# Room for four transpose tiles, another place for the first bias tiles, and an earlier fetch of the raw value weights at the end of a prologue

## The chip, the cores and the metric

The kernel runs on one core of one Trainium2 chip. The metric is the time of one execution in microseconds, as the device measures it; the median of several executions counts, and lower is better. Engines are called by name: TensorE (PE) multiplies matrices and transposes, VectorE (DVE), ScalarE (ACT) and GpSimd (POOL) do elementwise work, and SyncE (SP) issues most of the DMAs. All five run their own queue of instructions in order and meet through semaphores.

## The reference

One layer of a hybrid encoder, in float32, for a sequence of 2048 tokens of width 1024. The first norm feeds one projection; its first 512 columns go to a state-space layer, the rest are queries, keys and values of a chunked attention with a bias by relative distance.

```python
h = rmsnorm(x, norm_mix_g[l])
proj = h @ w_in[l]                      # 1024 -> u (512), q, k, v (512 each)
y_ssm = s5_mixer(u_ssm, lam, log_dt, b, c, d, w_glu, b_glu)
y_att = chunked_attention(q, k, v, rel_bias)     # 64-frame chunks, 8 chunks to the left
mixed = concat(rmsnorm(y_ssm, ...), rmsnorm(y_att, ...))
x = x + mixed @ w_out[l]
h2 = rmsnorm(x, norm_ffn_g[l])
x = x + (silu(h2 @ w_gate[l]) * (h2 @ w_up[l])) @ w_down[l]
return rmsnorm(x, norm_final_g)
```

## The kernel before

Everything is held feature by token: 128 features on the partitions, tokens along the row. Each float32 operand of a large product is split in two parts, `hi` (rounded) and `lo` (the rest), and a product is three matmuls (`mm3`): hi by hi, hi by lo, lo by hi. `split` makes the two parts of a weight: ScalarE casts `hi` out of a raw tile, VectorE or GpSimd subtracts it to get `lo`.

The stages follow one another: `u_phase` (the projection to u, in four pieces of 512 tokens, with the state-space constants of `ssm_prologue` computed between its steps), the attention with the state-space scan beside it (`att_phase`, four blocks of 512 tokens), the mixing, the gated FFN. Only the seam of the first two matters here, about 95 to 160 us into the run.

At that seam the following runs.

- `hT_unit(0)` loads the first block's input (`xt`, eight tiles of 128 by 512), scales it on VectorE and splits it into `hi` and `lo`. This happens in a callback `operands()` while TensorE still computes the last piece of u.
- VectorE then empties the last four accumulators of u (`us`), and GpSimd's queue writes them to memory (`u<-us`).
- `qk_unit(0, 0)` multiplies queries and keys of the first two heads (accumulators `pf`); its weights are tiles `w` split from `raw`.
- The rest of `ssm_prologue` follows: `bbg` and four `vg` are gathered from memory by SP, TensorE multiplies them (`pp<-vg,bbg`) into `kt`; then `transposes` turns the products `vw` in 16 pairs, ScalarE copies each pair to a tile `bst`, and GpSimd's queue writes each full `bst` (four pairs) to memory.
- `v_unit(0, 0)` multiplies values with weights n = 8 and n = 10; `scores` multiplies queries by keys into `sc`, adds the bias tile `nb` on VectorE and takes the minimum; `transp` turns the exponentials and stores them in `pth` and `ptl`.

The bias table `nbms` is written by `table()` from the small vector `nbs` and patched with `corner`; `nb` is one head's 128 by 640 piece of it.

What sets the order: TensorE's instructions, and those given through `k.V`, `k.A` and `k.Q` (VectorE, ScalarE, SyncE), keep their program order; the others are placed by a list scheduler. Tiles come from pools with a fixed count of buffers per tag (`bufs`). Two stacks of pools grow from both ends of the on-chip memory. A pool that is opened after another was closed lies over its room, and a write to a tile waits for every earlier reader and writer of the bytes below it. So the place of a tile decides what it waits for: `pk` (with `bst`, `vg`, `bbg`, `dm`, `kt`) lies over the tiles of `u_phase` on the right, and `aa` (with `nb`, `s`, `pth`, `ptl`) over those of the prologue (`vw` among them) on the left. Within `aa` the tiles lie in the order of their first use. All DMAs that SP issues go through one queue; each carries one of eight semaphores in turn and waits for the one eight before it.

Of the kernel before, what the change touches and what calls it, by code (L numbers as in the profile page):

```python
# [10 lines left out]
F32R = mybir.dt.float32r  # L11
# [5 lines left out]
P = 128  # L17
# [3 lines left out]
NG, CH, NS = 32, 16, 64  # L21
# [85 lines left out]
def f32(ap):  # L107
    return ap.bitcast(F32)
# [54 lines left out]
def split(k, hi, lo, raw, lo_eng=None, hi_eng=None):  # L163
    nc = k.nc
    (hi_eng or nc.scalar).copy(hi, raw)  # L165
    (lo_eng or nc.gpsimd).tensor_tensor(lo, raw, f32(hi), op=ALU.subtract)  # L166


def ssm_prologue(k, ident, S):

    tc, nc, io = k.tc, k.nc, k.io
    V = nc.vector
    with tc.tile_pool(name="pro", bufs=1) as p:
# [122 lines left out]
                eng.tensor_tensor(out, t1, t2, op=op)  # L296

        def transposes(pk, b_, wt):
            bst = k.t(pk, "bst", [P, 8, 2, NS], bufs=2)
            for q in range(4):  # L300
                ps = k.t(k.pro_psum, "pp", [P, 512])[:].rearrange("p (a b) -> p a b", a=4)
                for c in range(2):
                    k.te.transpose(ps[:, c, :], wt[c][:, q].rearrange("p j c -> p (j c)"), ident[:])
                nc.scalar.copy(bst[:, 2 * q : 2 * q + 2].rearrange("p g c n -> p c g n"), ps[:, :2].rearrange("p c (g n) -> p c g n", g=2))
                if q % 2:
                    yield
            nc.gpsimd.dma_start(S["bst"][b_], bst[:].rearrange("p g c n -> p (g c n)"))
# [8 lines left out]
        pr, pi = k.t(p, "pr", [P, NPR, 9]), k.t(p, "pi", [P, NPR, 9])  # L316
# [73 lines left out]
        pk = k.pk()  # L390
# [290 lines left out]
def att_phase(k, ident, S):  # L681
    tc, nc, io = k.tc, k.nc, k.io
    with ExitStack() as cx:
        aw = tc.alloc_tile_pool(name="aw", reuse_waits="tile", bufs=1, side="right")
        hT, vts, qk, keep = {}, {}, {}, {}

        def load_w(sb, n):

            w = k.t(aw, "w", [P, 2, 1024], F32R, bufs=WB)
            if sb == 0:  # L690
                raw = k.t(aw, "raw", [P, 1024], bufs=2)
                pin = n in (0, 4)
                (k.Q if pin else nc.sync).dma_start(raw[:], io["w_qk"][n] if n < 8 else io["w_v"][n - 8])
                split(k, w[:, 0], w[:, 1], raw[:], k.V if pin else k.wlo_eng, k.A if pin else None)
                keep[n] = w
            else:
                nc.sync.dma_start(f32(w[:]), S["ws"][n])
            return w[:, 0], w[:, 1]
# [5 lines left out]
        def hT_unit(sb, q0=0, q1=KT):  # L704
            hi, lo = hT.setdefault(sb, ([], []))
            ts = slice(sb * SB, (sb + 1) * SB)
            xts = {}
            V, A, Q = (k.V, k.A, k.Q) if sb == 0 else (nc.vector, nc.scalar, nc.sync)

            def load(q):  # L710
                if q < q1:
                    x = RING[q] if sb == 0 and q < 2 * DB else None
                    xts[q] = k.t(aw, x, [P, SB]) if x else k.t(aw, "xt", [P, SB], bufs=XB)
                    Q.dma_start(xts[q][:], io["xt"][q * P : (q + 1) * P, ts])

            ahead = 2 if sb else KT
            for q in range(q0, q0 + ahead):
                load(q)
            def low(q):
                V.tensor_tensor(lo[q][:], xts[q][:], f32(hi[q][:]), op=ALU.subtract)  # L720

            for q in range(q0, q1):
                yield
                load(q + ahead)
                xt = xts[q]
                for v, n in zip(hT[sb], ("hi", "lo")):
                    v.append(k.t(aw, f"{n}{q}x" if q < DB and sb % 2 else f"{n}{q}", [P, SB], F32R))
                V.scalar_tensor_tensor(xt[:], xt[:], k.gm[:, q : q + 1], S["rsn"][:, ts], op0=ALU.mult, op1=ALU.mult)
                A.copy(hi[q][:], xt[:])
                if sb == 0 and q:  # L730
                    low(q - 1)
                if sb or q == KT - 1:
                    low(q)
            yield

        def qk_unit(sb, pr):
            ws = [load_w(sb, n) for n in (pr, 4 + pr)]
            yield
            hi, lo = hT[sb]
# [42 lines left out]
        def v_unit(sb, fh):  # L782
            ws = [load_w(sb, 8 + 2 * r + fh) for r in range(2)]
            yield
            for i in range(4):
                vts[4 * sb + i, fh] = k.t(pv, f"v{fh}", [P, H // 2, 2 * HD], F32R)
            hi, lo = hT[sb]
            for i in range(4):
                ps = k.t(pfs, "pf", [P, 256])
                ic = slice(i * P, (i + 1) * P)  # L790
                for q in range(KT):
                    cs = slice((q % 4) * 256, (q % 4 + 1) * 256)
                    wh, wl = (w[:, cs] for w in ws[q // 4])
                    k.ta.matmul(ps[:], hi[q][:, ic], wh, start=q == 0, stop=False)
                    k.ta.matmul(ps[:], hi[q][:, ic], wl, start=False, stop=False)
                    k.ta.matmul(ps[:], lo[q][:, ic], wh, start=False, stop=q == KT - 1)
                    if q % 2 and q < KT - 1:
                        yield
                if i == 0:
                    for r in range(2):  # L800
                        keep_w(8 + 2 * r + fh)
                vt = vts[4 * sb + i, fh]
                pv3 = ps[:].rearrange("p (h d) -> p h d", h=4)
                nc.scalar.copy(vt[:, :, :HD], pv3)
                nc.vector.tensor_tensor(vt[:, :, HD:], pv3, f32(vt[:, :, :HD]), op=ALU.subtract)
                yield
# [45 lines left out]
        def transp(st):  # L852
            sb, pr, hh, qp = st
            hd = st_head[sb, 2 * pr + hh]
            if qp == 0:
                hd.p = k.t(aa, "pth", [P, 5, 4, P], F32R), k.t(aa, "ptl", [P, 5, 4, P], F32R)
            pth, ptl = hd.p
            s, k0 = hd.s.pop(qp)
            pt = k.t(psum, "pt", [P, 5, P], bufs=1)
            for kb in range(k0, qp + 5):  # L860
                k.ta.transpose(pt[:, kb % 5, :], s[:, (kb - k0) * P : (kb - k0 + 1) * P], ident[:])
            runs = [(0, 5)] if sb else ([(4, 5)] if qp == 0 else [(4, 5), (0, qp)])
            for a, b in runs:
                nc.scalar.copy(pth[:, a:b, qp, :], pt[:, a:b, :])
                nc.vector.tensor_tensor(ptl[:, a:b, qp, :], pt[:, a:b, :], f32(pth[:, a:b, qp, :]), op=ALU.subtract)
# [39 lines left out]
        def table():  # L905
            corner = k.t(aw, "corner", [64, 64])
            nc.gpsimd.memset(corner[:], 1e30)
            k.Q.dma_start(S["nbm"][:], bass.AP(S["nb"].tensor, S["nb"].offset + 1, [[768, H], [1, P], [1, 640]]))
            for m in range(2):
                k.Q.dma_start(S["nbm"][:, m * 64 : m * 64 + 64, m * 576 : m * 576 + 64].rearrange("h p c -> p h c"), corner[:].unsqueeze(1).to_broadcast([64, H, 64]))  # L910

        def operands():
            for _ in hT_unit(0):
                pass
            table()

        pro = u_phase(k, ident, S, aw, (lambda: next(first), operands))
# [8 lines left out]
        pps.release()  # L926
        pv = cx.enter_context(tc.tile_pool(name="av", reuse_waits="tile", bufs=8))
        aa = cx.enter_context(tc.tile_pool(name="aa", reuse_waits="tile", bufs=1))
        sp = tc.alloc_tile_pool(name="ssm", reuse_waits="tile", bufs=1)
        psum = cx.enter_context(tc.tile_pool(name="aps", bufs=1, space=bass.MemoryType.PSUM, reuse_waits="tile"))  # L930
        psum2 = cx.enter_context(tc.tile_pool(name="aps2", bufs=1, space=bass.MemoryType.PSUM, reuse_waits="tile"))
# [15 lines left out]
        for s in range(N + LAG + 2):  # L947
            if s == OPEN:
                aw.release()
                mix = mix_phase(k, S, lambda: k.t(pfs, "pf", [P, 512]))  # L950
                units += [Unit(islice(mix, MIX_N), MIX_N, GSTART, N + LAG, GSTART - OPEN)]
            if s == GSTART:
                sp.release()
            for o in ORDER:
                if o == "s" and s < N:
                    scores(steps[s])
                elif o == "t" and LAG <= s < N + LAG:
                    transp(steps[s - LAG])
                elif o == "p" and LAG + 1 <= s < N + LAG + 1 and steps[s - LAG - 1][3] == 3:
                    pv_head(steps[s - LAG - 1])  # L960
                elif o == "p" and s >= LAG + 2 and steps[s - LAG - 2][2:] == (1, 3):
                    pv_scale(steps[s - LAG - 2])
                elif o == "f":
                    for u in units:
                        u.advance(s)
# [739 lines left out]
```

## Time and profile before

| | us |
|---|---|
| three timed executions | 2327.14, 2330.36, 2331.63; median 2330.36 |
| the profiled execution: its own time | 2327.38 |
| its span on the core | 2325.6 |
| mean granted clock of TensorE | 0.971 of full speed |

Of the span TensorE is busy for 2191.2 us (94%), VectorE 1481.0, GpSimd 1130.8, ScalarE 1000.5. The profile has a page with busy times, shares and groups of instructions, and views that answer questions: a timeline of one engine (start, duration, engine, source line, operation, output<-inputs, size, count, and in brackets the idle time before it and what released it), a table by stretches of time (busy time of each engine, granted clock, DMA share and GB/s), and the DMAs by line with the median time from issue to landing. Line 88, 77, 74 and 166 are helpers (`Pinned`, `Ordered`, `split`), so instructions are best followed by the names of their tiles.

### The profile page before, as it was taken

To read this page: it belongs to the slowest core of one execution; us is meant where nothing else is said; L and a number is where in the kernel's file an instruction comes from. 1 tells how busy PE (TensorE), PEld (TensorE's weight loads), DVE (VectorE), ACT (ScalarE), POOL (GpSimd) and SP (SyncE) were. 2 spreads that over 40 slices of the span, in tenths; PEclk is the share of its full clock that TensorE was granted. 3 is DMA by queue.
4 is the path that set the end of the run, shared out by engine and by line. 5 is a ranking of instruction groups with operands and counts; after the bars stand their busy time and mean duration, and the time that the engine had idled before them with its cause. 6 is when DMAs were issued, how large, how long until landed. Compare 5 with 4: busy or idle time off the path is not lost.

```text
span 2325.6 us, 30451 instructions
## 1 busy us (share of the span) xinstructions
PE 2191.2 (94%) x10568; PEld 1839.8 (79%) x10568; DVE 1481.0 (64%) x2251; ACT 1000.5 (43%) x1675; POOL 1130.8 (49%) x1280
## 2 busy tenths in 40 slices
PE   8978899999997899989999998999999989999996
PEld 6667688898986788768888887788888778888886
DVE  7845555656556846666775667766645375578676
ACT  6335555555557542343333335333333343345322
POOL 3406645455660433565555558545555364445442
PEclk9989999999998999999999999999999999999998
DMA  8787766766643535644554556555433287465552
GB/s 296 256 280 259 226 206 199 213 194 193 187 139 114 177 122 170 227 160 149 167 192 162 195 195 239 195 194 167 156 95 110 87 321 251 163 219 181 202 186 73
DMA packets 214066, 437.00 MB, mean 188 GB/s; under 512 B 27096, under 2 KB 57864, under 8 KB 206808
## 3 DMA queue, kind: packets, MB, share of 16 engines
q1 hardware_dynamic: 209048, 420.89, 54.5%
q0 software_dynamic: 4864, 14.17, 1.9%
q8 instruction: 83, 1.36, 0.2%
q14 instruction: 71, 0.58, 0.1%
HBM read 294.98 MB, written 132.15 MB: 184 GB/s over the span
## 4 chain that ended last, share of the span: by engine, by line
PE 50%; DVE 3%; DMA 1%; issue 1%; POOL 1%; ACT 1%; SPq 0%; DVEq 0%; ACTq 0%; POOLq 0%
PE X L74 19%; PE ps L74 16%; PE Y L74 10%; PE W L74 5%; DVE sa L1554 1%; DVE lo L166 1%; DMA hd<-wc 1%; POOL c L166 0%; DMA acc<-x 0%; DVE S L1373 0%; DVE g L1438 0%; DMA hd<-hq 0%; DMA lo<-hc 0%; DVE acc L1571 0%; DVE u L1395 0%
## 5 line engine op out<-in xcount | busy, mean ns | idle before, releaser
L74 PE MATMUL X<-hi,c 128*128 128x512 f32 x1408 | 451.2, 391 | 9.1 <-ACT c L165 5.0
L74 PE MATMUL ps<-hd,hd 128*128 128x512 f32 (+1 forms) x1968 | 433.9, 382 | 7.7 <-POOL hd L166 5.4
L74 PEld LDWEIGHTS ps<-hd,hd 128*128 128x128 f32 x1968 | 359.9, 190 | 80.4 <-POOL hd L166 6.2
L166 POOL TENSOR_TENSOR c<-S,c 128x512 fp32r<-128x512 f32 x176 | 251.4, 1430 | 245.6 <-ACT c L165 244.6
L74 PEld LDWEIGHTS X<-hi,c 128*128 128x128 f32 x1408 | 265.4, 189 | 66.7 <-ACT c L165 5.4
L166 POOL TENSOR_TENSOR hd<-hd 128x1536 fp32r<-128x1536 f32 (+1 forms) x53 | 190.2, 3597 | 207.0 <-ACT hd L165 188.0
L74 PE MATMUL X<-lo,c 128*128 128x512 f32 x704 | 274.9, 390 | 0.0
L166 POOL TENSOR_TENSOR c<-raw,c 128x512 fp32r<-128x512 f32 x132 | 188.1, 1425 | 128.1 <-ACT c L165 100.6
L165 ACT CAST hd<-hd 128x1536 fp32r<-128x1536 f32 (+1 forms) x106 | 147.3, 1392 | 225.4 <-DMA hd<-hq 143.6
L74 PE MATMUL Y<-hi,c 128*128 128x512 f32 x704 | 227.2, 393 | 10.9 <-DVE u L1395 10.9
L1519 DVE TENSOR_TENSOR acc<-acc,ps 128x512 f32<-128x512 f32 x196 | 128.6, 681 | 80.8 <-PE ps L74 80.3
L74 PE MATMUL big<-m,woh 128*128 128x512 f32 x512 | 164.7, 402 | 1.9 <-DVE m L166 1.6
L74 PEld LDWEIGHTS Y<-hi,c 128*128 128x128 f32 x704 | 133.7, 190 | 40.5 <-DVE u L1395 12.6
L74 PE MATMUL pf<-hi,w 128*128 128x512 f32 x416 | 151.7, 417 | 7.3 <-ACT w L165 3.6
L165 ACT CAST c<-S 128x512 fp32r<-128x512 f32 x176 | 109.3, 622 | 111.9 <-PE Y L74 55.9
L605 POOL TENSOR_TENSOR st<-X,a 128x128 f32<-128x128 f32 (+2 forms) x136 | 47.0, 346 | 226.5 <-ACT X L591 164.8
L74 PEld LDWEIGHTS X<-lo,c 128*128 128x128 f32 x704 | 132.8, 189 | 27.4
L846 DVE CUSTOM_DVE_ANT_0 s<-sc,nb 128x640 f32<-128x640 f32 (+4 forms) x128 | 94.4, 738 | 93.3 <-PE sc L74 89.4
L1391 ACT COPY u<-X 128x512 f32<-128x512 f32 x132 | 77.1, 585 | 178.2 <-PE X L74 178.2
L165 ACT CAST c<-raw 128x512 fp32r<-128x512 f32 x132 | 82.1, 622 | 151.0 <-PE Y L74 81.3
L166 DVE TENSOR_TENSOR hd<-hd 128x1536 fp32r<-128x1536 f32 (+1 forms) x53 | 115.3, 2176 | 38.7 <-ACT hd L165 37.6
L74 PE MATMUL Y<-lo,c 128*128 128x512 f32 x352 | 138.2, 393 | 0.0
(463 smaller groups left out, 4693.5 us busy)
## 6 DMA issues: line engine op xcount, KB each, us to landing
w<-wss SPq DMA_DIRECT2D x36, 1024.0 KB, 5.7
hq<-g SPq DMA_DIRECT2D x140, 256.0 KB, 2.0
hd<-hq SPq DMA_DIRECT2D x42, 768.0 KB, 4.5
hd<-wc SPq DMA_DIRECT2D x42, 768.0 KB, 6.1
raw<-in_w_gate SPq DMA_DIRECT2D x44, 512.0 KB, 3.6
raw<-in_w_up SPq DMA_DIRECT2D x44, 512.0 KB, 4.2
wc<-px SPq DMA_DIRECT2D x66, 256.0 KB, 2.9
wss<-w SPq DMA_DIRECT2D x12, 1024.0 KB, 5.8
```

Of the source, the lines that this page charges most:

```text
L74: return self.tc.keep_in_program_order(self.tc.nc.tensor.matmul(*a, **b))
L165: (hi_eng or nc.scalar).copy(hi, raw)
L166: (lo_eng or nc.gpsimd).tensor_tensor(lo, raw, f32(hi), op=ALU.subtract)
L605: eng.tensor_tensor(t[:, :, :, :n], src, ar, op=ALU.mult)
L846: nc.vector.tensor_tensor_reduce(s[:, :nk].rearrange("p (a b) -> p a b", a=nch), ps[:, :nch, :half], hd.nb[:, nk - 1 :: -1].rearrange("p ( ...
L1391: nc.scalar.copy(u[:], ps[:])
L1519: V.tensor_tensor(a, a, ps[:], op=ALU.add)
L1554: (nc.gpsimd if m else nc.vector).tensor_tensor(self.sa[m][:, :n], self.sa[m][:, :n], t[:, :n], op=ALU.add)
```

## The change

It does three things. `transposes` asks for four `bst` tiles and not two. The raw weights of the first value unit (n = 8 and 10) are loaded in `operands()`, right after the first block's input and ahead of the bias table, by a pinned DMA of SP; `load_w` then takes the tile that is there. And the first `pth` and `ptl` are asked for ahead of everything else in the pool `aa`, so that they get its first bytes, and `nb` and `s` lie behind them.

```diff
         def transposes(pk, b_, wt):
-            bst = k.t(pk, "bst", [P, 8, 2, NS], bufs=2)
+            bst = k.t(pk, "bst", [P, 8, 2, NS], bufs=4)
...
+        raws = {}
+
+        def load_raw(n, dma):
+            raw = raws[n] = k.t(aw, "raw", [P, 1024], bufs=2)
+            dma(raw[:], io["w_qk"][n] if n < 8 else io["w_v"][n - 8])
+
         def load_w(sb, n):
 
             w = k.t(aw, "w", [P, 2, 1024], F32R, bufs=WB)
             if sb == 0:
-                raw = k.t(aw, "raw", [P, 1024], bufs=2)
                 pin = n in (0, 4)
-                (k.Q if pin else nc.sync).dma_start(raw[:], io["w_qk"][n] if n < 8 else io["w_v"][n - 8])
+                if n not in raws:
+                    load_raw(n, (k.Q if pin else nc.sync).dma_start)
+                raw = raws.pop(n)
                 split(k, w[:, 0], w[:, 1], raw[:], k.V if pin else k.wlo_eng, k.A if pin else None)
...
             if qp == 0:
-                hd.p = k.t(aa, "pth", [P, 5, 4, P], F32R), k.t(aa, "ptl", [P, 5, 4, P], F32R)
+                hd.p = (k.t(aa, "pth", [P, 5, 4, P], F32R), k.t(aa, "ptl", [P, 5, 4, P], F32R)) if (sb, pr, hh) != (0, 0, 0) else p0
...
         def operands():
             for _ in hT_unit(0):
                 pass
+            for n in (8, 10):
+                load_raw(n, k.Q.dma_start)
             table()
...
         aa = cx.enter_context(tc.tile_pool(name="aa", reuse_waits="tile", bufs=1))
+        p0 = tuple(k.t(aa, n, [P, 5, 4, P], F32R) for n in ("pth", "ptl"))
```

SP's queue at the seam, before, from the last input tile to the first store of a weight; in brackets the semaphores that a row waits for (DMASW: a DMA that GpSimd's queue issued, DMAHW: one of SP's own, the others by engine):

```order
L88 DMA xt_1222<-in_xt 128x512 [waits DMAHW6_49,DVE_49]
L88 DMA nbms_69<-nbs_70 1024x1x640 [waits DMAHW7_49]
L396 DMA bbg_1468<-bbs_79 128x32x16 [waits DMASW2_49,DMASW3_49,DMASW1_49,DMAHW0_49,DMASW0_49,PE_49]
L403 DMA vg_1472<-vs_72 128x8x128 [waits DMASW2_49,DMASW3_49,DMASW1_49,DMAHW1_49,DMASW0_49,PE_49]
L88 DMA nbms_69<-corner_1264 64x8x64 [waits DMAHW7_49,DMAHW2_49,Pool_49]
L88 DMA nbms_69<-corner_1264 64x8x64 [waits DMAHW3_49]
L403 DMA vg_1474<-vs_72 128x8x128 [waits DMASW6_49,DMASW7_49,DMASW5_49,DMAHW4_49,DMASW4_49,PE_49]
L403 DMA vg_1476<-vs_72 128x8x128 [waits DMASW7_49,DMASW6_49,DMAHW5_49,DMASW1_49,DMASW0_49]
L403 DMA vg_1478<-vs_72 128x8x128 [waits DMASW3_49,DMASW2_49,DMAHW6_49,DMASW1_49,DMASW0_49]
L88 DMA wss_75<-w_1153 128x2048 [waits DVE_49]
```

And now:

```order
L88 DMA xt_1222<-in_xt 128x512 [waits DMAHW6_49,DVE_49]
L88 DMA raw_1264<-in_w_v 128x1024 [waits DMAHW7_49,DVE_49]
L88 DMA raw_1266<-in_w_v 128x1024 [waits DMAHW0_49,DVE_49]
L88 DMA nbms_69<-nbs_70 1024x1x640 [waits DMAHW1_49]
L396 DMA bbg_1472<-bbs_79 128x32x16 [waits DMASW3_49,DMASW4_49,DMASW2_49,DMASW6_49,DMASW1_49,DMAHW2_49,DMASW0_49,DVE_49]
L403 DMA vg_1476<-vs_72 128x8x128 [waits DMASW3_49,DMASW1_49,DMAHW3_49,DMASW0_49,PE_49]
L88 DMA nbms_69<-corner_1268 64x8x64 [waits DMAHW4_49,DMAHW1_49,Pool_49]
L88 DMA nbms_69<-corner_1268 64x8x64 [waits DMAHW5_49]
L403 DMA vg_1478<-vs_72 128x8x128 [waits DMASW7_49,DMAHW6_49,DMASW5_49,PE_49]
L403 DMA vg_1480<-vs_72 128x8x128 [waits DMASW7_49,DMAHW7_49,DMASW1_49,DMASW0_49]
```

The two raw loads stand ahead of `nbms`; they wait for VectorE, which frees their buffers with the low halves of the query and key weights. `bbg` lay over operands of u and waited for TensorE; it lies over `us` tiles of the last u piece now, and waits for VectorE and for more writes of GpSimd's queue: DMASW2 here is the write of the third of the four last `us` tiles.

VectorE's queue where the first block's operands are made; the scaling rows are `hi0x` and `lo0x`, the low halves `lo`:

```order
 L88 SCALAR_TENSOR_TENSOR hi0x_1208<-hi0x_1208,g_mix_88,rsn_94 128x512
 L88 SCALAR_TENSOR_TENSOR lo0x_1210<-lo0x_1210,g_mix_88,rsn_94 128x512
+L166 TENSOR_TENSOR w_1524<-raw_1264,w_1524 128x1024
 L88 TENSOR_TENSOR lo_358_1225<-hi0x_1208,hi_357_1224 128x512
 L88 SCALAR_TENSOR_TENSOR hi1x_1212<-hi1x_1212,g_mix_88,rsn_94 128x512
```

The low half of the first value weight has moved up from behind the last `kt` step to a place ahead of the first operand's low half. On ScalarE its cast stands ahead of the first operand's cast in the same way; the second value weight's cast stands behind the second of the 16 `bst` copies, where it stood behind the eleventh.

## Prediction

> **What bounds the kernel now.** I read the page first, then TensorE's timeline between 100 and 165 us, then the same stretch for the other engines and for SP's queue, and last the granted clock and the DMA share stretch by stretch.
>
> ```profile
> PE 2191.2 (94%) x10568; PEld 1839.8 (79%) x10568; DVE 1481.0 (64%) x2251; ACT 1000.5 (43%) x1675; POOL 1130.8 (49%) x1280
> ```
>
> TensorE is busy for 94% of the span, so a microsecond that its first stage loses or gains is carried to the end. The change touches only the end of the prologue. There TensorE's timeline (start, duration, what ran, and in brackets the idle time before it and what ended that) reads:
>
> ```profile
> 112.23 0.40 PE L74 MATMUL pf<-hi,w 128*128 128x512 f32 x1
> ...
> 123.23 1.92 PE L74 MATMUL pp<-vg,bbg 128*16 128x128 f32 x16
> 125.75 5.41 PE L74 MATMUL pp<-vg,bbg 128*16 128x128 f32 x48 [0.59 <-DMA vg<-vs]
> 131.09 3.29 PE L77 MATMUL pp<-ident,vw 128*128 128x128 f32 x28
> 141.88 1.12 PE L77 MATMUL pp<-ident,vw 128*128 128x128 f32 x4 [7.51 <-ACT bst L304]
> 144.10 0.48 PE L74 MATMUL sc<-hi2x,hi0x 128*128 128x128 f32 x1 [1.10 <-ACT bst L304]
> ...
> 153.79 0.55 PE L74 MATMUL sc<-hi2x,hi0x 128*128 128x256 f32 x1 [3.98 <-DVE mn L846]
> ```
>
> Two waits stand out: 7.51 us inside the prologue's transposes, and 3.98 us before the second score product. ScalarE's rows tell where the first comes from: eight copies into `bst`, a cast that waits for the raw value weights, then 4.54 us for the `bst` DMA, because only two `bst` tiles exist.
>
> ```profile
> 131.68 2.21 ACT L304 COPY bst<-pp 128x256 f32<-128x256 f32 x8
> 135.88 1.04 ACT L165 CAST w<-raw 128x1024 fp32r<-128x1024 f32 x1 [1.99 <-DMA raw<-in_w_v]
> 141.46 0.92 ACT L304 COPY bst<-pp 128x256 f32<-128x256 f32 x3 [4.54 <-DMA bsts<-bst]
> ```
>
> The second comes from the bias tile. SP issues `nb` at 145.02, behind everything before it, and the median landing of `nb` is 8.0 us, so about 153.0; VectorE's first score step runs at 153.35.
>
> ```profile
> 145.02 0.71 SPq L817 DMA_DIRECT2D nb<-nbms  x1
> ```
>
> ```profile
> nb<-nbms SPq DMA_DIRECT2D x2, 320.0 KB, 8.0
> ```
>
> ```profile
> 153.35 0.29 DVE L846 CUSTOM_DVE_ANT_0 s<-sc,nb 128x128 f32<-128x128 f32 x1 [2.67 <-POOL XG L634]
> ```
>
> The waits cost more than their length. The table by stretch has busy time of PE, PEld, DVE, ACT and POOL, then the granted clock, the DMA share and GB/s:
>
> ```profile
> 134.50:139.10 4.60, 0.00 (x0) 0.00 (x0) 1.23 (x1) 1.04 (x1) 0.23 (x1) 1.00 1.02 327
> 139.30:141.80 2.50, 0.00 (x0) 0.00 (x0) 0.00 (x0) 0.34 (x2) 0.00 (x0) 0.50 1.06 423
> 144.10:149.40 5.30, 5.30 (x25) 5.30 (x26) 0.48 (x1) 0.77 (x3) 0.86 (x2) 0.50 0.89 330
> 149.90:152.80 2.90, 0.00 (x0) 0.00 (x0) 0.42 (x1) 0.32 (x1) 0.00 (x0) 1.00 1.02 349
> 153.80:159.60 5.80, 5.80 (x27) 5.80 (x28) 2.41 (x4) 1.93 (x5) 0.00 (x0) 0.50 0.88 347
> ```
>
> The clock falls to 0.50 after nearly 5 us of idleness and after 3 us, and the products behind both waits run at half speed for 5.3 and 5.8 us, which loses half of that, 2.65 and 2.9 us. And while TensorE waits, the DMA engines do not:
>
> ```profile
> 97.00:109.00 12.00, 12.00 (x54) 9.72 (x53) 11.97 (x19) 4.36 (x7) 2.20 (x4) 1.00 0.63 229
> 109.00:119.00 10.00, 10.00 (x45) 8.22 (x44) 9.70 (x17) 0.62 (x1) 5.23 (x9) 1.00 0.92 263
> ...
> 121.00:144.00 23.00, 13.90 (x107) 11.35 (x105) 10.21 (x17) 11.99 (x28) 3.34 (x7) 0.90 1.05 372
> 144.00:145.00 1.00, 0.90 (x4) 0.91 (x5) 0.58 (x1) 0.87 (x4) 0.42 (x1) 0.50 0.34 143
> 145.00:153.00 8.00, 4.81 (x24) 4.60 (x23) 0.42 (x1) 0.37 (x1) 0.53 (x1) 0.71 1.01 356
> ```
>
> From 121 to 153 their share is 1.0 with one hole of a microsecond. So the second score product hangs on a backlog of transfers, not only on the engine named beside it.
>
> **The raw value weights, earlier.** They leave a saturated stretch (SP issued them at 126.26, median landing 10.2) for one at a share of 0.63.
>
> ```profile
> 95.39 2.36 DVE L88 TENSOR_TENSOR w<-raw,w 128x1024 fp32r<-128x1024 f32 x2
> ...
> 101.49 0.69 DVE L88 TENSOR_TENSOR lo<-hi0x,hi 128x512 fp32r<-128x512 f32 x1
> ...
> 110.47 2.65 DVE L88 TENSOR_TENSOR us<-ps,pb 128x512 f32<-128x512 f32 x4
> ...
> 116.30 0.67 DVE L398 TENSOR_TENSOR dm<-ident,ddt 16x512 f32<-16x512 f32 x1
> ```
>
> ```profile
> 126.26 2.18 SPq L693 DMA_DIRECT2D raw<-in_w_v  x2
> ```
>
> ```profile
> raw<-in_w_v SPq DMA_DIRECT2D x2, 512.0 KB, 10.2
> xt<-in_xt SPq DMA_DIRECT2D x2, 256.0 KB, 4.2
> ```
>
> Their buffers come free with the two `w` splits, so the first goes out at 95.39 + 1.23 = 96.6. Its landing lies between the 4.2 us of an `xt` half its size at the same place and 10.2; I take 4.5, since the share is the `xt` row's. It is there at 101.1. But its split now stands in the queues of ScalarE and VectorE ahead of the first block's operands: the cast (1.04) ends at 102.1, the low half (1.23) at 103.4, and the low half of the first operand, at 101.49 before, starts about D = 1.8 us later. D is 1.2 if the landing is early and 7.6 if it takes 10.2. VectorE has no idle time there (11.97 of 12.00), so all of D reaches the four `us` steps at 110.47. The query/key products at 112.23 need the bank that the first of them empties: it was ready at 110.47 + 0.66 = 111.1, so 1.1 us of slack; TensorE starts 0.7 us later. `nbms`, which stood next on SP's queue, goes out later at no cost of its own: the row behind it waits until 108.24 anyway.
>
> **Four tiles for the transposes.** The second wait on a `bst` tile goes: 16 copies of 0.28 (2.21 / 8) and one cast of 1.04 follow each other in 5.5 us. But two more tiles make the pool larger, and its other tiles lie elsewhere: in the built program `bbg` no longer waits for TensorE alone, but for the write of a `us` tile to memory, and `dm` for another.
>
> ```profile
> 111.45 1.74 POOL L505 DMA_DIRECT2D u<-us  x3 [10.47 <-DVE us L88]
> ```
>
> ```profile
> 108.24 0.39 SPq L396 DMA_DIRECT2D bbg<-bbs  x1
> 108.94 9.97 SPq L403 DMA_DIRECT2D vg<-vs  x1
> ...
> 120.59 3.01 SPq L403 DMA_DIRECT2D vg<-vs  x3
> ```
>
> ```profile
> u<-us POOLq DMA_DIRECT2D x4, 256.0 KB, 5.3
> bbg<-bbs SPq DMA_DIRECT2D x1, 256.0 KB, 12.0
> ```
>
> The third `u` write goes out at 111.45 + 2 x 0.58 + D = 114.4 and lands 5.3 later: `bbg` leaves at 119.7 and not at 108.24, 11.5 us later. Behind it on SP stand `vg`, the two corners, three more `vg`, the weight stores and all that follows. Before, `vg` sat 9.97 us in its issue, until 118.9, which is 10.7 after `bbg`'s start; `bbg` then shared the engines with `nbms` and the `u` writes (share 0.92 in that stretch). Now it comes after them. What it takes alone no row shows: not below the 4.2 of an `xt` of its size (less 0.7 of its own issue: 3.5 until `vg` is out), not above 10.7. I take 5.5, nearer the lower end, because the traffic beside it is gone. `vg` is out at 125.2, so SP's queue runs 6.3 us late (4.3 to 11.5). `dm` may wait 1 us for its `u` write, which VectorE's later slack before the `kt` steps covers.
>
> [...]
>
> The first `kt` products then come at about 122.6 + 6.3 = 128.9 and not 123.23, a new wait of nearly 5 us, and the 48 behind the second `vg` start at 125.75 + 6.3 = 132.0 and end at 137.4. Of the transposes' 11.9 us (131.09 to 143.0) some 5.5 remain. The first score product needs the thirteenth copy: 137.4 + 0.6 + 13 x 0.28 + 1.04 = 142.7, against 144.10. So 7.5 us of waiting go, 6.3 come back, and this point gains 1.4.
>
> **The first bias tile's place.** `nb` no longer waits for the last transposes. It still stands on SP behind both stores of the value weights. There are two bounds. By the chain of engines, the second value weight is split at 138.0 + 0.56 + 1.04 + 1.23 = 140.8, `nb` goes out at 141.2 and lands at 149.2, 3.8 earlier than the 153.0 of before. By the backlog, the same transfers start 6.3 later, without the two raw loads (1 MB at 372 GB/s: 2.8) and without the hole of 144 to 145 (0.7): 153.0 + 6.3 - 2.8 - 0.7 = 155.8. I take 154.5, close to the backlog, because the share was 1.05 all that time. TensorE is done with the first value products by 149 at the latest and waits again; its clock falls again and the half-speed stretch of 5.8 us stays. The second score product comes 1.5 us later than before.
>
> **The sum.** The profiled execution took 2327.38 us; 2327.4 + 1.5 = 2328.9. It lies 3.0 below the median of the three timed runs (2330.36), and all four average 2329.1, so for a fresh median I say 2329.1 + 1.5 = 2330.6: no difference that can be seen. What a measurement of this kernel can tell from no change is about 0.2%, 4.7 us.
>
> **Rivals.** *The stalls simply go (faster).* If `bbg` takes 3.5 us and the backlog does not bind, the queue is 4.3 late, the `kt` products end 2 us sooner and `nb` lands near 147.2. [...] For it: 1 MB less in the full stretch. Against it: share 1.05 for 23 us. It decides where `nb` lands before 149. [...]
>
> *The new wait on the `u` writes costs more than the old one (slower).* The place is `bbg` on SP's queue. If its 4096 runs of 64 bytes cost by themselves what they cost before (10.7 until `vg` is out), the queue is 11.5 late, the `kt` products end at 142.6, and the backlog puts `nb` at 153.0 + 11.5 - 2.8 - 0.7 = 161.0: 8 us, so 2337.1. For it: the one row that there is says 12.0. It decides above a shift of some 9 us.
>
> *The early split blocks the operands (slower).* With a landing of 10.2, D is 7.6; every step behind it, `bbg` included, moves by 5.8 more: 2336.4. Against it: the share of 0.63.
>
> **How the numbers follow.** Forecast, within 0.2%: 0.53, its own range 2326 to 2335. The stalls go: 0.19. The two slower rivals together: 0.28, the first of them 0.2. The range that leaves out some 2 in 10 reaches into both sides: 2322 to 2338.
>
> **What would show it.** Right: the row of `bbg` on SP near 120; idle time of about 5 us before the first `kt` products, released by `vg`; no wait between the transposes; the first score product at 142 to 144; `nb` landing at 153 to 156, with the clock at 0.50 on both sides of the second score product. Wrong: `bbg` near 108, `us` still at 110.5, `nb` landing before 149, or a `vg` that sits in its issue for 10 us again.

## The result, and the profile after

The changed kernel takes 2333.14 us (median of 22 runs, 2325.95 to 2338.51), the kernel before 2328.72 us beside it (22 runs); the ratio is 1.0018, 95% interval 1.0009 to 1.0026. A second measurement on another occasion gave 2330.24 us (12 runs) against 2329.44 us (35 runs), ratio 1.0004, interval 0.9991 to 1.0017. Both ratios lie within the 0.2% that the forecast took as the least that can be told from no change. The first lies on the slow side by more than its interval, whose end is above 0.2%; the second doesn't differ from 1. The forecast was 2330.6 us, range 2322 to 2338.

The profiled execution of the changed kernel happens to be the fastest of its 22 (2325.95 us; before 2327.38), so its total says nothing; what it shows is the seam. TensorE's timeline there:

```profile
114.76 0.47 PE L74 MATMUL pf<-hi,w 128*128 128x512 f32 x1 [0.98 <-DVE us L88]
...
128.53 1.91 PE L74 MATMUL pp<-vg,bbg 128*16 128x128 f32 x16 [2.64 <-DMA vg<-vs]
130.87 1.92 PE L74 MATMUL pp<-vg,bbg 128*16 128x128 f32 x16 [0.42 <-DMA vg<-vs]
...
139.15 2.37 PE L77 MATMUL pp<-ident,vw 128*128 128x128 f32 x16 [0.53 <-ACT bst L304]
141.90 0.33 PE L74 MATMUL sc<-hi2x,hi0x 128*128 128x128 f32 x1 [0.39 <-ACT bst L304]
...
155.32 0.56 PE L74 MATMUL sc<-hi2x,hi0x 128*128 128x256 f32 x1 [10.06 <-DVE mn L853]
```

The wait of 7.51 us between the transposes is gone, and the first score product comes 2.2 us earlier (144.10 before). But the wait before the second score product has grown from 3.98 to 10.06 us, and that product comes 1.5 us later (153.79 before). Of these 1.5 us 1.3 are not the change's: this execution was that much later already ahead of it (the experiments come back to this). SP's queue, and the DMAs that matter (count, size, and median microseconds from issue to landing):

```profile
122.17 0.38 SPq L396 DMA_DIRECT2D bbg<-bbs  x1
122.74 2.13 SPq L403 DMA_DIRECT2D vg<-vs  x1
...
126.50 2.78 SPq L403 DMA_DIRECT2D vg<-vs  x3
...
142.19 1.27 SPq L824 DMA_DIRECT2D nb<-nbms  x1
```

```profile
raw<-in_w_v SPq DMA_DIRECT2D x2, 512.0 KB, 6.2
nb<-nbms SPq DMA_DIRECT2D x2, 320.0 KB, 11.9
...
bbg<-bbs SPq DMA_DIRECT2D x1, 256.0 KB, 4.0
```

`bbg` goes out at 122.17 and not at 108.24, but lands in 4.0 us and not in 12.0, and `vg` no longer sits in its issue (2.13 against 9.97). `nb` goes out 2.8 us earlier than before, but lands later. The 11.9 us (8.0 before) are not those of this load: of the two `nb` loads the view knows the landing of the second only. The first, on which the score step waits, lands at 154.7 by the trace's semaphore updates, 12.5 us after its issue (before at 153.2, after 8.2 us), and VectorE's first score step follows.

```profile
96.70 2.36 DVE L88 TENSOR_TENSOR w<-raw,w 128x1024 fp32r<-128x1024 f32 x2
...
104.96 0.68 DVE L88 TENSOR_TENSOR lo<-hi0x,hi 128x512 fp32r<-128x512 f32 x1
113.93 2.48 DVE L88 TENSOR_TENSOR us<-ps,pb 128x512 f32<-128x512 f32 x4
...
154.87 0.29 DVE L853 CUSTOM_DVE_ANT_0 s<-sc,nb 128x128 f32<-128x128 f32 x1 [8.74 <-DMA nb<-nbms]
```

The clock, in stretches (busy time of PE, PEld, DVE, ACT, POOL, then granted clock, DMA share, GB/s):

```profile
145.30:155.20 9.90, 0.00 (x0) 0.00 (x0) 0.72 (x3) 0.37 (x1) 0.11 (x1) 0.65 1.01 394
155.30:157.70 2.40, 2.38 (x11) 2.40 (x12) 0.79 (x3) 1.88 (x5) 0.00 (x0) 0.50 1.04 413
157.70:159.20 1.50, 1.50 (x12) 1.50 (x12) 1.37 (x2) 0.11 (x2) 0.00 (x0) 0.73 0.47 178
```

It falls within the idle time (0.65 on the mean of 145.30 to 155.20), as before. The first value products ran at 0.50 before and run at full speed now, as the stretch below shows, but since TensorE then waits for `nb` anyway, that buys nothing.

```profile
142.20:145.20 3.00, 3.00 (x26) 2.86 (x24) 0.00 (x0) 0.48 (x2) 0.73 (x2) 1.00 1.03 425
```

### The profile page after: what moved, and what is told of

It reads as the page before. It is cut to its first block, busy times and chain, and to the rows that moved or that the text cites. A ratio compares the mean times of both kernels' runs of the same rounds, so it can differ in the third digit from the quotient of the medians.

```text
span 2324.2 us, 30449 instructions
## 1 busy us (share of the span) xinstructions
PE 2183.0 (94%) x10568; PEld 1832.8 (79%) x10568; DVE 1484.4 (64%) x2251; ACT 1000.3 (43%) x1675; POOL 1133.4 (49%) x1280
## 4 chain that ended last, share of the span: by engine, by line
PE 52%; DVE 2%; POOL 1%; DMA 1%; issue 1%; ACT 0%; DVEq 0%; SPq 0%; POOLq 0%; ACTq 0%
PE X L74 19%; PE ps L74 19%; PE Y L74 9%; PE W L74 5%; DVE lo L166 1%; POOL c L166 0%; DMA lo<-hc 0%; DMA hd<-wc 0%; DVE S L1383 0%; DVE acc L1581 0%; DVE g L1448 0%; POOL lo L166 0%; DVE u L1405 0%; DVE hd L166 0%; POOL hd L166 0%
## 5 line engine op out<-in xcount | busy, mean ns | idle before, releaser
L74 PE MATMUL X<-hi,c 128*128 128x512 f32 x1408 | 451.3, 391 | 10.7 <-ACT c L165 6.2
L1529 DVE TENSOR_TENSOR acc<-acc,ps 128x512 f32<-128x512 f32 x196 | 128.9, 681 | 83.6 <-PE ps L74 83.3
```

Of the source, the lines that this page charges most:

```text
L74: return self.tc.keep_in_program_order(self.tc.nc.tensor.matmul(*a, **b))
L1529: V.tensor_tensor(a, a, ps[:], op=ALU.add)
```

## The experiments

The **first score step** (VectorE's first row that reads `nb`, 153.35 us before) is the mark by which the kernels are compared; it ends the seam. "Second vg" is the start of the row of three `vg` on SP (120.59 before), from which the stores and all the seam's later transfers follow.

| kernel | second vg | first score step | against before | ratio to before, 95% interval |
|---|---|---|---|---|
| changed kernel | 126.50 | 154.87 | +1.5 | 1.0018, 1.0009 to 1.0026 |
| the same again (a2) | 125.61 | 153.54 | +0.2 | 1.0004, 0.9991 to 1.0017 |
| e1 four tiles alone | 121.86 | 150.96 | -2.4 | 0.9990, 0.9977 to 1.0002 |
| e2 early fetch alone | 124.12 | 153.39 | 0.0 | 1.0001, 0.9990 to 1.0011 |
| e3 bias place alone | 120.02 | 152.78 | -0.6 | 0.9999, 0.9986 to 1.0012 |
| e4 whole change, added tiles below | 123.73 | 153.88 | +0.5 | 1.0003, 0.9993 to 1.0013 |
| e5 change without the early fetch | 122.08 | 151.48 | -1.9 | 0.9996, 0.9981 to 1.0010 |
| e6 change, nb by GpSimd's queue | 124.58 | 156.25 | +2.9 | 1.0021, 1.0009 to 1.0034 |
| e7 e5 with nb by GpSimd's queue | 121.76 | 150.99 | -2.4 | 1.0008, 0.9996 to 1.0021 |
| e8 e6 with small stores (work left out) | 125.41 | 155.24 | +1.9 | 1.0015, 0.9999 to 1.0031 |
| e9 tiles below, no early fetch | 119.30 | 148.54 | -4.8 | 0.9982, 0.9969 to 0.9996 |
| e9 again (e11) | 121.39 | 151.02 | -2.3 | 0.9989, 0.9974 to 1.0005 |
| e10 change, one store early | 127.17 | 154.80 | +1.5 | 1.0011, 1.0001 to 1.0022 |

Over these 13 rows the ratio follows the first score step (correlation 0.89, a slope of 1.1 us of run time for 1 us at the seam). One step of one profiled execution varies by 1.3 to 2.5 us between two executions of one kernel (rows 1 and 2, e9 and e11), and a ratio by about 0.1%, so a single row proves little, e7's above all; the column as a whole agrees with the view that what the seam gains or loses reaches the end.

Part of that spread comes from ahead of the seam. VectorE's split of the query and key weights, which the change doesn't touch, starts at 95.39 before, but at 96.70 in the changed kernel, 95.64 in the same program's other execution (a2), 94.65 in e2, 94.92 in e4, 94.59 in e9 and 95.50 in e11. Net of that, the first score step of the changed kernel stands at +0.2 and -0.1 against before, that of e2 at +0.8, of e4 at +1.0, of e9 at -4.0 and -2.4. So at the end of the seam the change is worth nothing either way, and the 0.18% of its first measurement is not explained by the seam; where it comes from stays open.

**Each part alone (e1, e2, e3).** The four tiles:

```diff
-            bst = k.t(pk, "bst", [P, 8, 2, NS], bufs=2)
+            bst = k.t(pk, "bst", [P, 8, 2, NS], bufs=4)
```

> The four bst tiles alone, nothing else of the change. By my theory (the larger pool lays bbg over a us tile, so SP waits for a u write): bbg on SP at 119 to 121 and not at 108.24, no wait between the transposes, the first kt products near 128 and not 123.23. The raw value weights stand behind that queue, so the first value products come some 6 us late, near 148 to 150; the second score product near 155 to 157; 1 to 4 us slower than before. By the rival that the early raw loads are what costs: bbg may move, but the time is that of before or 2 to 5 us better, because the transposes no longer stall.

SP's rows and VectorE's step in e1:

```profile
117.08 0.39 SPq L396 DMA_DIRECT2D bbg<-bbs  x1
117.64 2.58 SPq L403 DMA_DIRECT2D vg<-vs  x1
...
121.86 3.57 SPq L403 DMA_DIRECT2D vg<-vs  x3
```

```profile
150.96 0.29 DVE L846 CUSTOM_DVE_ANT_0 s<-sc,nb 128x128 f32<-128x128 f32 x1 [3.55 <-DMA nb<-nbms]
```

`bbg` waits for the u write (the "u wait" from here on) as expected (117.08, 2 us before the expected window), but the wait moves the second `vg` by only 1.3 us: the first `vg` sits 2.58 us in its issue and not 9.97. The kernel isn't slower, as my theory had it, but 0.1% faster, which its interval doesn't separate from none. A miss of the theory, in favour of the rival. One thing more differs: in e1, as in e5 and e9, the scheduler puts `nb` between the two value weights' stores and not behind both. No run moves `nb` there and changes nothing else, so how much of the lead of these kernels is that place stays open; the section on queue or engines comes back to it.

The early fetch alone keeps two `bst` tiles and the bias tile's place:

```diff
+            for n in (8, 10):
+                load_raw(n, k.Q.dma_start)
             table()
```

> The early fetch of the raw value weights alone; two bst tiles and the bias tile's place as before. By my theory: the value weights' split stands ahead of the first block's operands and delays VectorE's chain by about 2 us; bbg at 109 to 111; the stalls between the transposes stay; nb still waits for the last transposes and lands at 152 to 155; the time within 2 us of before. By the rival (the early raw loads are what costs): 3 us or more slower than before, already in the stretch ahead of 123 us.

SP's queue, the transposes, and the stretch behind in e2:

```profile
97.99 0.79 SPq L88 DMA_DIRECT2D nbms<-nbs  x1
107.50 1.11 SPq L396 DMA_DIRECT2D bbg<-bbs  x1
108.83 13.62 SPq L403 DMA_DIRECT2D vg<-vs  x1
...
124.12 3.58 SPq L403 DMA_DIRECT2D vg<-vs  x3
```

```profile
143.79 1.11 PE L77 MATMUL pp<-ident,vw 128*128 128x128 f32 x4 [4.93 <-ACT bst L304]
```

```profile
120.00:124.00 4.00, 3.61 (x16) 2.64 (x15) 3.88 (x6) 0.89 (x2) 0.00 (x0) 1.00 0.60 96
```

The delay of VectorE is there, the stall too, and the time is that of before, as expected. What was not expected: `vg` sits 13.62 us in its issue and not 9.97, so the second `vg` is 3.5 us late without any u wait, and behind that the engines run nearly dry: 96 GB/s from 120 to 124, where before they moved 270:

```profile
120.00:124.00 4.00, 4.00 (x22) 3.10 (x21) 3.86 (x7) 1.17 (x2) 0.00 (x0) 1.00 1.05 270
```

What holds `vg` is, by these rows, `bbg` (`vg` is out at 122.45, about 1 us ahead of its landing at 123.5; 1.3 us ahead before and in the changed kernel, 1.2 in e9), and what slows `bbg` more than before is, as far as the trace shows, the bias table. Before, the table goes out 2.7 us earlier:

```profile
95.28 0.79 SPq L88 DMA_DIRECT2D nbms<-nbs  x1
```

The trace also records every DMA packet with its queue, size and start. The table's 1024 packets of 2560 bytes run from 97.4 to 115.3 before, but from 101.8 to 120.1 in e2, behind those of the two raw loads; `bbg`'s packets of 64 bytes run among them and end 3 to 5 us after them (at 119.95 and 123.2). While SP sits at `vg` its queue starts nothing else (before, `vg` is out at 118.91 and the next row starts at 119.01). The later stretch makes the delay good: with a megabyte less in it the first score step is back where it was before, so in this build the early fetch neither gains nor costs.

The bias place alone:

```diff
+        p0 = tuple(k.t(aa, n, [P, 5, 4, P], F32R) for n in ("pth", "ptl"))
```

> The bias tile's place alone: nb no longer waits for the last transposes. By my theory nb then goes out right behind the store of the second value weight, 2 to 4 us earlier than before, and lands at 149 to 152 (before 153.0); the second score product 1 to 3.5 us earlier than 153.79; time 0 to 4 us below before. If the DMA backlog alone sets the landing: nb lands at 153 as before, and the time does not change.

```profile
152.78 0.29 DVE L846 CUSTOM_DVE_ANT_0 s<-sc,nb 128x128 f32<-128x128 f32 x1 [2.22 <-DMA nb<-nbms]
```

The first score step comes at 152.78, 0.6 us earlier, and the time stays: less than my theory expected, near what the backlog alone would give. `nb` goes out at 144.88, hardly earlier than the 145.02 of before, since the issue of the two stores ahead of it ends at 144.79 only. Before, the step's row named not `nb` but `XG` on GpSimd, a tile cleared at 153.14 after the last `bsts` write; by the trace `nb` landed at 153.2 too, so two waits ended there within 0.1 us. Here `nb` alone is left.

**The whole change without the u wait (e4).** The two added tiles get a tag of their own that is asked for first, so that they lie lowest and the others where they lay before:

```diff
         pk = k.pk()
+        more = [k.t(pk, "bsm", [P, 8, 2, NS], bufs=2) for _ in range(2)]
...
-            bst = k.t(pk, "bst", [P, 8, 2, NS], bufs=4)
+            bst = more[b_ - 2] if b_ > 1 else k.t(pk, "bst", [P, 8, 2, NS], bufs=2)
```

> The whole change, but with the two added bst tiles requested first in the pool, so that they lie below the others, and kt, bbg, dm, vg and the first two bst lie where they lay before. By my theory (the wait on the u write costs what the transposes gain): bbg on SP at 109 to 111, no stall between the transposes, the first kt products at 123 to 126, the first score product at 136 to 139 (142.7 forecast and 141.90 seen with the whole change), nb landing at 147 to 151, the second score product 4 to 8 us earlier than 155.32; time 2 to 8 us below the changed kernel, at or below before. By the rival that the DMA backlog alone binds: nb still lands at 153 to 156 and the time is that of the changed kernel.

```profile
107.77 0.80 SPq L397 DMA_DIRECT2D bbg<-bbs  x1
108.80 13.26 SPq L404 DMA_DIRECT2D vg<-vs  x1
```

```profile
139.67 0.33 PE L74 MATMUL sc<-hi2x,hi0x 128*128 128x128 f32 x1 [0.39 <-ACT bsm L304]
...
154.33 0.55 PE L74 MATMUL sc<-hi2x,hi0x 128*128 128x256 f32 x1 [11.29 <-DVE mn L854]
```

The u wait is gone and the first score product comes at 139.67, but the second only at 154.33, 11.29 us of idle time later, and the time is that of before. The rival is closer here: what comes earlier in the engines here waits for DMAs. But two of them: `nb`, issued at 140.1, lands at 152.5 by the trace's semaphore updates, 0.9 to 2.2 us ahead of the changed kernel's two, and then the first score step, at 153.88, waits 1.4 us more for the write of an added tile (its row names `bsts<-bsm`, issued at 140.74, as what came last).

**Without the early fetch (e5), beside the changed kernel again (a2).** e5 is the change without `load_raw` in `operands()`.

> The changed kernel once more, beside the others on one chip. Its first profiled execution (2325.95 us) was the lowest of its 22 runs, and it showed the first score step only 0.3 us later than before from 180 us on. By the theory that the seam (the stretch from 95 to 165 us) sets the whole difference: median 0 to 2 us above before. By the rival that the early raw loads and the u wait together cost more in a common execution than in that one: 3 to 5 us above before, with the first score step 3 us or more behind that of before.

> The four bst tiles and the bias tile's place, without the early raw loads. In this build nb stands between the stores of the two value weights, and not behind both. By the theory that the early raw loads cost what the other two parts gain: bbg at 117, second vg near 122 (126.50 with the whole change), first score step at or before 151, 3 to 6 us below the changed kernel and 1 to 4 us below before. By the rival that the u wait under bbg is what costs: as slow as the changed kernel.

a2 fits the first theory (median 0.8 us above before, first score step 0.2 us behind). e5 has its second `vg` at 122.08 and its first score step at 151.48, 2.1 to 3.4 us ahead of the changed kernel's two, as expected of the early fetch as the cost. The time misses the expectation: the ratios (0.9996 and 1.0004) lean the same way but overlap, and by the medians e5 (2331.11) is 0.9 us slower than a2 (2330.24). And the place of `nb` between the stores differs too, so e5 alone doesn't show that the early fetch is the cost.

**Queue or engines (e6, e7, e8).** The first bias tile is fetched by GpSimd's queue:

```diff
+        nbs[0] = load_nb(0, nc.gpsimd)
```

> The whole change, but the first bias tile nb is fetched through GpSimd's queue, behind the four bsts writes and not behind the stores of the value weights on SP. By the theory that nb waits for its place in the queue: it goes out at 144 and lands at 147 to 151 (154.1 with the whole change), TensorE's idle time before the second score product falls from 10.06 to 3 to 7 us, time 2 to 6 us below the changed kernel. By the rival that the DMA engines are full and any transfer takes as long: it lands at 153 to 156, no gain.

> As the kernel without the early raw loads, with nb fetched through GpSimd's queue too. By the theory of the queue: nb lands at 147 to 150, first score step 1 to 4 us earlier than with nb between the two stores; 2 to 6 us below before. By the rival of full DMA engines: no difference from the kernel without the early raw loads.

e6's issue and landing of `nb`:

```profile
142.20 0.55 POOL L824 DMA_DIRECT2D nb<-nbms  x1
```

```profile
nb<-nbms POOLq DMA_DIRECT2D x1, 320.0 KB, 13.9
```

In e6 `nb` no longer stands behind the two stores, goes out at 142.20, and takes 13.9 us; e6 is 0.2% slower than before. In e7 it goes out at 138.65 and takes 12.2, and the first score step (150.99) is that of e5. That another queue would be faster falls. But e6 and e7 keep `nb` in the same place, behind the four `bsts` writes, and differ in the early fetch alone: with it the first score step comes at 156.25, without it at 150.99, and the means of 12 runs each differ by 5.0 us (95% interval 2.7 to 7.1). Here the early fetch does cost, at the seam and in the time. The same tile, fetched between 160 and 250 us in the changed kernel, takes 4.0:

```profile
nb<-nbms SPq DMA_DIRECT2D x4, 320.0 KB, 4.0
```

So it isn't slow by itself; at the seam (12.5 us) it waits among other transfers. The packets show for which: in the changed kernel `nb`'s first packet starts at 150.0, when 95% of the packets of 8192 bytes of the two stores ahead of it on SP's queue have started (149.8); in e6 it starts at 152.5, when 95% of those of the four `bsts` writes and what else went ahead of it on GpSimd's queue have (152.4). On either queue some 2 MB stand ahead of `nb` (two stores of 1 MB, four writes of 512 KB), and both queues move data at once: by the packets that start between 142 and 150 in the changed kernel, SP's moved 2.2 MB and GpSimd's 1.2.

e8 then takes traffic away: of the stores of weights 0, 4, 8 and 10 only 64 of 1024 columns are written, and the second block reads other copies.

```diff
+                c = 64 if n in (0, 4, 8, 10) else 1024
-                (k.Q if n in (0, 4) else nc.sync).dma_start(S["ws"][n], f32(keep.pop(n)[:]))
+                (k.Q if n in (0, 4) else nc.sync).dma_start(S["ws"][n][:, :, :c], f32(keep.pop(n)[:, :, :c]))
```

> As the kernel with nb on GpSimd's queue (e6), but of each of the four weight stores of the seam (numbers 0, 4, 8 and 10, 1 MB each) only 64 of 1024 columns are written, and the second block loads the copies of four other weights in their place: some 3.75 MB of traffic go, the output isn't the reference's. nb goes out behind the same four bsts writes, with the same waits. By the theory that the DMA engines' backlog sets its landing (13.9 us from issue to landing in e6): 4 to 8 us from issue to landing, the second score product at 145 to 150 and not at 156.69, the time 4 to 9 us below e6. By the rival that this transfer is slow by itself (its rows are read from a table written shortly before): 12 to 14 us again, no gain.

```profile
nb<-nbms POOLq DMA_DIRECT2D x1, 320.0 KB, 13.4
```

```profile
136.00:140.00 4.00, 3.68 (x32) 3.27 (x31) 0.75 (x3) 4.00 (x15) 2.17 (x4) 1.00 0.91 243
...
144.00:148.00 4.00, 0.00 (x0) 0.00 (x0) 1.67 (x3) 0.00 (x0) 0.00 (x0) 0.89 1.04 418
148.00:152.00 4.00, 0.00 (x0) 0.00 (x0) 0.75 (x1) 0.00 (x0) 0.11 (x1) 0.50 1.03 430
```

Still 13.4: the theory in this form missed. The engines have some room up to 140 (243 GB/s at a share of 0.91), but right then four `bsts` writes of 512 KB stand ahead of `nb` in the same queue, and SP fills the freed place with later loads (raw weights and inputs, from 137 on), so that they are full again from 144 on (418 GB/s at 1.04). The stores alone are thus not what `nb` waits for. By the packet records its first one starts at 150.8, when 95% of those ahead of it on its own queue have started (150.9): it stands behind the `bsts` writes, and SP's traffic runs beside these. No run takes either away alone.

**One store into the hole (e10).** While SP waits for the u write, the engines move 207 to 208 GB/s (108 to 116 in the changed kernel); the store of weight 8 is sent there through GpSimd's queue. The hole in the changed kernel's table of stretches, and the edit:

```profile
108.00:112.00 4.00, 4.00 (x19) 3.20 (x18) 4.00 (x8) 2.07 (x4) 0.00 (x0) 1.00 0.51 207
112.00:116.00 4.00, 3.02 (x14) 2.17 (x13) 3.91 (x7) 0.65 (x2) 1.03 (x2) 1.00 0.52 208
```

```diff
-                (k.Q if n in (0, 4) else nc.sync).dma_start(S["ws"][n], f32(keep.pop(n)[:]))
+                (k.Q if n in (0, 4) else nc.gpsimd if n == 8 else nc.sync).dma_start(S["ws"][n], f32(keep.pop(n)[:]))
```

> The whole change, but the first value weight's store (1 MB) goes through GpSimd's queue right behind its split near 105, while SP waits for the u write, and not through SP at 139. By the backlog theory it fills the stretch in which the DMA engines are half idle (208 GB/s from 108 to 116 in the changed kernel), so that nb lands 1 to 3 us earlier than with the whole change (152.9 and 154.1 seen); time 1 to 3 us below the changed kernel. By the rival that the hole is no real capacity: the u writes behind it come late, bbg goes out after 124, and nothing is gained.

```profile
104.03 0.54 POOL L709 DMA_DIRECT2D wss<-w  x1 [2.46 <-DVE w L166]
```

It goes out at 104.03, but `bbg` stays at 121.54, its landing takes 5.1 us and the `u` writes' 7.5 (6.6 in the changed kernel), the second `vg` comes at 127.17, and the first score step at 154.80. No gain; closer to the rival, though `bbg` did not come later than 124. The store filled little of the hole: it went out 4 us ahead of it, the engines moved 381 GB/s from 104 to 108 (309 in the changed kernel) but only 220 from 108 to 112, and the bias table's packets end at 124.5 and not at 120.7. So this edit says little on whether the hole can be used.

**The version that follows (e9).** Four tiles, the added two below, the bias place, no early fetch:

> Four bst tiles with the two added ones below the others (no u wait), the bias tile's place, no early raw loads. By the theory that the early raw loads delay bbg and vg (13.26 us in the issue of the first vg in e4, 9.97 before): bbg at 108, second vg at 120 to 121, no wait between the transposes, first score step at 149 to 151, 1 to 4 us below before. By the rival that only the backlog counts and the queue's place does not: as e5, first score step at 151.5.

> e9 once more, unchanged, since its lead over before (0.9982, interval 0.9969 to 0.9996) is as large as the difference of two measurements of one kernel. By the theory that the earlier second score product (148.99 against 153.79) is what it gains: first score step again at 148 to 151, ratio 0.997 to 0.9995. If the first measurement was luck of the later stages: first score step early, ratio at 1.0 within its interval.

```profile
107.43 0.39 SPq L397 DMA_DIRECT2D bbg<-bbs  x1
108.12 9.49 SPq L404 DMA_DIRECT2D vg<-vs  x1
...
119.30 3.19 SPq L404 DMA_DIRECT2D vg<-vs  x3
```

```profile
120.00:124.00 4.00, 4.00 (x26) 3.13 (x26) 3.86 (x7) 1.17 (x2) 0.00 (x0) 1.00 1.11 310
```

```profile
148.99 0.55 PE L74 MATMUL sc<-hi2x,hi0x 128*128 128x256 f32 x1 [6.36 <-DVE mn L847]
```

No u wait, no stall between the transposes, no hole (the first score product now waits 4.12 us for the value weights' split): 310 GB/s from 120 to 124, and the second score product at 148.99 against 153.79 before and 155.32 with the change. 2326.46 us (12 runs), 0.9982 of before; again 2327.61 us, 0.9989. It has the lowest ratios of the study, and is faster than before in the first measurement beyond its interval, in the second not. The second execution's first score step (151.02) is that of e1 and e5, as the rival said, so a gain of the added tiles' place over theirs is not shown.

## Why the prediction was right, step by step

**The early fetch and VectorE's delay D.** The profiled execution runs 1.3 us later already ahead of the change (the two low halves of the query and key weights start at 96.70, 95.39 before). The first operand's low half starts at 104.96, 3.5 after 101.49, so D is 2.2 us; 1.8 was taken. The rival that the early split blocks the operands (7.6) falls: ScalarE's cast, which waits for the first of the two raw loads, starts at 102.73, 4.8 us after that load's issue at 97.95; 4.5 was taken. (The 6.2 of the view is the second load's.)

**`bbg` and the u wait.** `bbg` at 122.17, forecast 119.7; 1.3 of the 2.5 us are the late start. From its start until `vg` is out 2.7 us pass (122.74 + 2.13 - 122.17). I took 5.5 between bounds of 3.5 and 10.7: mis-sized, and below even the lower bound. `bbg` lands in 4.0 us once the bias table is through, and `vg` was out 1.3 us ahead of that landing, before as now, where I had taken 0.7. The rival that the new wait costs more than the old (10.7 until `vg` is out) falls by the same number.

**SP's queue.** Forecast 6.3 us late, measured 5.9 (126.50 against 120.59) and 5.0 in the second execution; 4.6 and 4.8 net of the late start. The sum was near, its parts were not: this is the step that failed. I put all of it down to the u wait and held that `nbms` goes out later "at no cost of its own". The runs give the u wait 1.3 to 1.5 us (e1, e5) and the early fetch 3.5 (e2), because the later table holds `bbg` and with it `vg`; together 4.8 to 5.0. That the two mistakes cancel is luck. The other half held: 2.8 us for the early megabyte and 0.7 for the hole were to come back in the later backlog, and in e2 3.5 us had come back at the first score step.

**The products and the transposes.** First `kt` products 128.53 (128.9 forecast), no wait of more than 0.53 us between the transposes, first score product 141.90 (142.7). The gain at that point is 2.2 us, not 1.4. The wait before the `kt` products is 2.64 us and not nearly 5, since TensorE began the query/key products 2.5 us later than before (114.76), not 0.7.

**The bias tile.** Of the two bounds, engine chain (149.2) and backlog (155.8), I took 154.5, close to the backlog; it landed at 154.7, in the second execution at 153.4. The kind is shown by e4 and e6: `nb` issued earlier or by another queue still lands at 152.5 and 156.1. The second score product came 1.5 us later, the number that was forecast, and 0.2 later in the second execution (153.99). But 1.3 and 0.25 of these were there ahead of the seam; net of that the product didn't move, so the match is luck, and the +1.5 was about 1.5 too much.

**The clock.** It fell again, as forecast; the half-speed stretch behind the second score product was not the 5.8 us of before, but about 3.2 (0.50 up to 157.7, and 0.73 on the mean of the next 1.5), and over 3.9 in the second execution.

```profile
154.00:157.90 3.90, 3.90 (x18) 3.90 (x19) 1.15 (x3) 1.97 (x5) 0.11 (x1) 0.50 1.03 411
```

So this price was 5.8, about 3.2 and over 3.9 us of half speed in three executions; no run here tests what sets its length. The difference is worth up to 1.3 us (half of 2.6), of which the forecast knew nothing.

**The sum.** +1.5 us was forecast; the medians differ by +4.4 and +0.8. In both profiled executions the seam ends within 0.2 us of before, net of its start. So "no difference" was right by the mechanism (what the engines gain, 2.2 us at the first score product, the DMAs take back), but the +1.5 itself has no support, and the +4.4 of the first measurement stays unexplained. The rival that the stalls simply go falls: e4 has neither the transposes' stall nor the u wait and gains nothing, because DMAs set the end of the seam there (`nb` lands at 152.5, and the step at 153.88 waits for a `bsts` write).

## What to carry to other kernels

A stall that a buffer count causes is worth only what lies between it and the next late thing (here 7.51 us of stall went, and the second score product came no earlier): look up the DMA share in the stretch behind it first, and if it is full, ask what a change does to the order and the start of transfers, not to the engines. Where pools lie over each other, a larger pool moves its neighbours onto other tiles and so onto other waits (`bbg` from 108.24 to 122.17); asking for the new tiles first left the waits of `bbg` and `vg` as they were, but gave the first score step a new one (e4). And an early fetch is no gift where one queue issues in order: count what it holds up behind it (3.5 us at the second `vg` in e2), not only what it takes out of the later stretch.

## What the hardware showed that was not expected

A gather of 256 KB in runs of 64 bytes (`bbg`) took 4.0 to 5.1 us where it went out behind the u writes, 11.2 to 12.9 among the `nbms` and `u` writes, and 15.5 and 16.0 when the raw loads' megabyte had put the table back (e4, e2). It landed 4.9 us after the table's last packet before and 3.4 in e2. Issuing it 8.8 us later (e1) cost the queue behind it only 1.3 us.

A 320 KB load took 4.0 us where the DMA share was 0.69 on the mean (160 to 250 us) and 7.7 (e3) to 14.2 (e6) at the seam, on SP's queue as on GpSimd's (12.5 and 13.9), and 3.75 MB less of stores shortened it by 0.5 us only (13.9 to 13.4). Its first packet started when 95% of those ahead of it on its own queue had: at 150.0 against 149.8 in the changed kernel, 152.5 against 152.4 in e6, 150.8 against 150.9 in e8.
